# The last addition of the rotary step and the sums of the branch projections on VectorE instead of GpSimd

## The chip, the core and the metric

The kernel runs on one core of a Trainium2 chip. The core has a matrix engine (TensorE, PE in the rows, with its weight loads as PEld), VectorE (DVE), ScalarE (ACT), GpSimd (POOL) and a queue that issues the DMAs (SyncE, SP). Each engine works through its own list of instructions in order, and semaphores make one engine wait for another. The metric is the time of one execution on the device in microseconds (us), as the median of several runs.

## What is computed

Two layers of a transformer trunk over 256 tokens of width 1024, all in float32. A layer has a mixer and a mixture of experts (MoE). Cut to what matters here:

```
h = rms_norm(x) * (1 + scale_m(c)) + shift_m(c)
z = h @ w_in                       # q, k, v of three attention branches, and three gates per channel
q, k = apply_rotary(q), apply_rotary(k)      # branches A and C:  x*cos + rotate_half(x)*sin
o_a, o_n, o_d = diff_attention, neighbourhood_attention, dilated_attention
merged = sum over i of sigmoid(gate_i) * (o_i @ w_proj_i)
x = x + gate_m(c) * (merged @ w_out)
h = rms_norm(x) * (1 + scale_f(c)) + shift_f(c)
x = x + gate_f(c) * hier_moe(h)    # 32 experts in 8 groups of 4
```

The six vectors scale, shift and gate of a layer come from silu(c) @ ada_w, which is another large weight matrix to be read.

## The kernel before

**The work.** `mixer` computes z in 15 chunks of 512 columns (`chunk(n)`). A chunk's weights come in two tiles of 1 MB. They are used as pairs of a rounded part and a remainder: `split` makes the rounded part `whi` with ScalarE (L302) and the remainder `wlo` with VectorE (L303), four times a chunk, and `gemm` adds up three products for each (hi*whi, hi*wlo, lo*whi). So PE can't go on in a quarter of a chunk before VectorE has made its `wlo`. Chunks 0 to 8 hold q, k and v, chunks 9 to 14 the gates. Ten pieces of q and k in each layer need the rotary step, `place`: four shifted copies by ScalarE (L461), two products by VectorE (L462, which reads the matmuls' PSUM bank, and L463), and one addition (L464).

**Around it.** During the chunks the modulation vectors are made too: `ada_part` loads 1 MB of ada_w, and VectorE multiplies and adds it up in two instructions on 128x1024 (L166, each followed by a short one that fetches the sum). The attention of the three branches (`diff_attention`, `na_attention`, `dil_attention`) is written ahead of the gate chunks, and the scheduler lays both into each other on PE. A dilated block consists of scores (matmuls into a `misc` bank), a masked maximum by VectorE (L659), an exponential by ScalarE (L661), a scaling by VectorE (L662, L663), four transposes by PE (L560) with a copy by ScalarE (L562), and the product with v; two heads go through together. Then come the projections of the branches (two halves of 512 columns, three branches each), where VectorE multiplies each with its gate (L493) and adds the branches up (L495; in the first half on GpSimd, in the second on VectorE), and `w_out`.

**The MoE.** For each group of four experts eight tiles of 2 MB (`w13`, L718) and four of 2 MB (`w2g`, L735) are loaded and used once. All weights of the kernel pass through one pool of ten pairs of tiles of 2 MB in all; the DMA queue is in order, and a load starts when its tile has been read by whoever used it before.

**The order.** The program is written as above, but a scheduler orders each engine's instructions before the kernel runs, by a model of the time that each takes. Which instruction stands ahead of which on PE, VectorE and ScalarE is thus decided at build time, with the engine that an addition runs on as an input.

The two statements that the change touches are these (`d` and `sh` are 128x512 in SBUF, `m` and `g` too):

```
nc.vector.tensor_mul(v(d), v(z), cos)             # L462
nc.vector.tensor_mul(v(sh), v(sh), sin)           # L463
nc.gpsimd.tensor_add(d, d, sh)                    # L464
...
nc.vector.scalar_tensor_tensor(g if bi else m, g, 1.0, o[i], op0=OP.add, op1=OP.mult)   # L493
if bi:
    (nc.vector if half else nc.gpsimd).tensor_add(m, m, g)                              # L495
```

Of the kernel before, what the change touches and what calls it, by code (L numbers as in the profile page):

```python
# [53 lines left out]
def bc(ap, at, n):  # L54

    a = [list(e) for e in ap.ap]
    a.insert(at, [0, n])
    return bass.AP(tensor=ap.tensor, offset=ap.offset, ap=a)


class Kernel:
# [288 lines left out]
    def mixer(self, l, fill):  # L350

        nc, tc, io = self.nc, self.tc, self.io
# [37 lines left out]
        def work(name):  # L390
            T, o, n = {"E": (T0, 0, 3), "A": (T1, 0, 2), "PT": (T1, 1024, 2), "PD": (T1, 0, 4)}[name]
            i = turn.get(name, 0)
            turn[name] = (i + 1) % n
            return T[:, o + 512 * i:o + 512 * (i + 1)]
# [22 lines left out]
        def chunk(n):  # L417
# [11 lines left out]
            for kind, c0, wd, dst in SEGS[n]:  # L429
                if wd == 512:  # L430
                    z = [self.acc(), self.acc()]
                    prods += self.wide(z)
                    evac += [lambda t=t, z=z, kind=kind, dst=dst:
                             nc.scalar.copy(vdst[kind][:, t, dst:dst + 512], z[t]) for t in range(2)]
                    continue
                z = self.acc()
                if kind in vdst:
                    prods += [(z[:, t * 256:(t + 1) * 256], False, t, slice(c0, c0 + 256), t == 0) for t in range(2)]
                    evac.append(lambda z=z, kind=kind, dst=dst: nc.scalar.copy(
                        vdst[kind][:, :, dst:dst + 256], z.rearrange("p (t n) -> p t n", t=2)))  # L440
                    continue
                prods += self.flipped(z, c0)
                if kind == "g":
                    evac.append(lambda z=z, dst=dst: nc.scalar.activation(ga[dst // 2], z, AF.Tanh, scale=0.5))
                else:
                    evac.append(lambda z=z, kind=kind, dst=dst: place(z, kind, (qT2 if kind[1] == "q" else kT2)[dst]))
# [6 lines left out]
        def place(z, kind, d):  # L453
            if kind[0] == "n":
                nc.scalar.mul(d, z, 0.125 if kind == "nq" else 1.0)
                return
            cos, sin = (bc(self.rope[:, i, :], 1, 2) for i in range(2))
            v = lambda a: a.rearrange("p (a n) -> p a n", a=2)
            sh = work("PD")
            for q in range(4):  # L460
                nc.scalar.copy(sh[32 * q:32 * q + 32], z[32 * (q ^ 1):32 * (q ^ 1) + 32])  # L461
            nc.vector.tensor_mul(v(d), v(z), cos)  # L462
            nc.vector.tensor_mul(v(sh), v(sh), sin)  # L463
            nc.gpsimd.tensor_add(d, d, sh)  # L464

        for n in range(9):
            chunk(n)
# [15 lines left out]
        for half in range(2):  # L483
            w = [self.slot().rearrange("p (k n) -> p k n", k=4) for _ in range(2)]
            for b in range(2):
                nc.sync.dma_start(w[b], io["w_proj"][l, half, b].rearrange("p (k n) -> p k n", k=4))
            for bi, (k0, nk) in enumerate(srcs):
                o = [self.acc(), self.acc()]
                self.gemm([(k, w[k // 4][:, k % 4:k % 4 + 2]) for k in range(k0, k0 + nk, 2)], hi, lo,
                          self.flipped(o[0], 0) + self.flipped(o[1], 256))  # L490
                for i in range(2):
                    g, m = ga[4 * bi + 2 * half + i], tok[half][:, 512 * i:512 * (i + 1)]
                    nc.vector.scalar_tensor_tensor(g if bi else m, g, 1.0, o[i], op0=OP.add, op1=OP.mult)  # L493
                    if bi:
                        (nc.vector if half else nc.gpsimd).tensor_add(m, m, g)  # L495
        hi, lo = self.to_hilo(None, [tok[i // 2][:, 512 * (i % 2):512 * (i % 2 + 1)].rearrange(
            "p (a n) -> p a n", a=2) for i in range(4)])
        self.gate_row(l, 0)
# [612 lines left out]
```

## Time and profile before

| | |
|---|---|
| median of 3 runs | 1509.85 us (1509.48 to 1510.61) |
| the profiled execution | 1507.89 us |
| its span, first to last instruction | 1506.0 us |
| PE busy | 1198.5 us (80%) |
| VectorE busy | 614.6 us (41%) |
| ScalarE busy | 372.2 us (25%) |
| GpSimd busy | 57.5 us (4%), 67 instructions |
| read from HBM | 542 MB, 361 GB/s over the span |
[...]

The stages follow one another: the first modulation vectors until about 37 us, the mixer of layer 0 until about 332, the MoE of layer 0 until about 774, the mixer of layer 1 until about 1057, the MoE of layer 1 until the end. The share of the span that an engine is busy is a mean over stages of two kinds, so the profile has to be read stage by stage.

### The profile page before, as it was taken

How to read it: one execution, taken by the hardware profiler on the slowest of the kernel's cores; microseconds unless marked ns; L12 is line 12 of the kernel's file. 1: busy time of each engine (PE TensorE's matmuls, PEld its weight loads, DVE VectorE, ACT ScalarE, POOL GpSimd, SP SyncE). 2: the span in 40 equal slices, each digit the busy share in tenths (PEclk: the TensorE clock that was granted, in tenths of full speed). 3: DMA queues.
4: the chain of work that ended last, by engine and by line, in shares of the span. 5: the costliest groups of instructions: out<-in, count | busy, mean ns of one | idle time of the engine just before them, and what ended most of it. 6: DMA issues, size and time to landing. Idle time of an engine off the chain costs nothing. (4 is left out here: it accounts for less than half of the span.)

```text
span 1506.0 us, 19652 instructions
## 1 busy us (share of the span) xinstructions
PE 1198.5 (80%) x8146; PEld 787.0 (52%) x8146; DVE 614.6 (41%) x1246; ACT 372.2 (25%) x664; POOL 57.5 (4%) x67
## 2 busy tenths in 40 slices
PE   2999998989877676676778999999787578577675
PEld 2898987874333132231358989889443133133132
DVE  6889974572121021110149997457322112022012
ACT  2765554350000000000046656544100000000001
POOL 0102000100000000000001110010000000000001
PEclk7999998899988897897999999999998888798898
DMA  9887971769999999999996965276999999999997
GB/s 373 351 348 279 380 293 57 298 254 390 427 428 427 427 427 428 429 427 428 424 416 280 390 276 221 113 284 247 365 426 429 426 430 426 427 429 427 429 428 296
DMA packets 53084, 544.43 MB, mean 362 GB/s; under 512 B 7168, under 2 KB 8192, under 8 KB 12160
## 3 DMA queue, kind: packets, MB, share of 16 engines
q1 hardware_dynamic: 52992, 543.13, 86.9%
q8 instruction: 66, 1.08, 0.3%
q14 instruction: 26, 0.21, 0.0%
HBM read 542.04 MB, written 1.06 MB: 361 GB/s over the span
## 5 line engine op out<-in xcount | busy, mean ns | idle before, releaser
L95 PE MATMUL acc<-rg,xg 128*32 128x512 f32 x2048 | 282.0, 694 | 115.6 <-DMA rg<-w 113.5
L95 PE MATMUL acc<-rg,b 128*32 128x512 f32 (+1 forms) x1152 | 153.0, 662 | 95.9 <-DMA rg<-w2g 69.2
L95 PEld LDWEIGHTS acc<-rg,xg 128*32 128x32 f32 x2048 | 68.6, 119 | 304.3 <-issue 295.1
L95 PE MATMUL acc<-hi,wlo 128*128 128x256 f32 x704 | 200.2, 289 | 7.9 <-DVE wlo L303 7.7
L95 PE MATMUL acc<-lo,whi 128*128 128x256 f32 x704 | 196.1, 284 | 0.0
L95 PE MATMUL acc<-hi,whi 128*128 128x256 f32 x704 | 191.4, 286 | 1.2 <-ACT whi L302 1.1
L303 DVE TENSOR_TENSOR wlo<-rg,whi 128x1024 fp32r<-128x1024 f32 x116 | 145.0, 1250 | 59.1 <-ACT whi L302 58.1
L813 DVE TENSOR_TENSOR b<-b,acc 128x512 f32<-128x512 f32 x16 | 11.0, 688 | 353.1 <-PE acc L95 353.1
L302 ACT CAST whi<-rg 128x1024 fp32r<-128x1024 f32 x116 | 121.5, 1047 | 107.4 <-PE acc L95 99.2
L95 PEld LDWEIGHTS acc<-hi,wlo 128*128 128x128 f32 x704 | 135.1, 192 | 15.3 <-DVE wlo L303 11.6
L95 PEld LDWEIGHTS acc<-rg,b 128*32 128x32 f32 x1152 | 33.9, 120 | 197.1 <-DMA rg<-w2g 105.1
L95 PEld LDWEIGHTS acc<-lo,whi 128*128 128x128 f32 x704 | 134.5, 192 | 1.4 <-issue 1.0
L95 PEld LDWEIGHTS misc<-b,xn 128*128 128x128 f32 x512 | 124.6, 334 | 16.9 <-issue 15.5
L95 PEld LDWEIGHTS acc<-hi,whi 128*128 128x128 f32 x704 | 131.0, 192 | 2.9 <-ACT whi L302 2.1
L95 PE MATMUL misc<-b,xn 128*128 128x128 f32 x512 | 125.6, 404 | 3.9 <-DVEq L918 2.0
L166 DVE CUSTOM_DVE_ANT_0 rg<-rg,grb 128x1024 f32<-128x1024 f32 x96 | 118.6, 1274 | 10.0 <-DMA rg<-ada_w 9.8
L812 ACT ACTIVATE b<-acc 128x512 f32<-128x512 f32 x16 | 9.6, 597 | 440.7 <-PE acc L95 440.7
L826 DVE TENSOR_TENSOR Y<-acc,grb 128x512 f32<-128x512 f32 x28 | 19.4, 692 | 228.2 <-PE acc L95 228.2
L793 DVE TENSOR_SCALAR xg<-misc,mcol 128x128 f32<-128x128 f32 x128 | 44.3, 405 | 106.5 <-PE misc L95 106.5
L806 ACT COPY b<-misc 128x256 f32<-128x256 f32 x16 | 6.0, 373 | 329.2 <-PE misc L805 329.2
L95 PE MATMUL acc<-hi,rg 128*128 128x256 f32 x384 | 74.6, 293 | 13.1 <-ACT hi L265 12.1
L95 PEld LDWEIGHTS acc<-hi,rg 128*128 128x128 f32 x384 | 62.7, 201 | 14.4 <-ACT hi L265 12.6
(168 smaller groups left out, 1437.0 us busy)
## 6 DMA issues: line engine op xcount, KB each, us to landing
rg<-w SPq DMA_DIRECT2D x128, 2048.0 KB, 39.1
rg<-w2g SPq DMA_DIRECT2D x56, 2048.0 KB, 38.9
rg<-w_in SPq DMA_DIRECT2D x56, 1024.0 KB, 9.8
rg<-ada_w SPq DMA_DIRECT2D x48, 1024.0 KB, 8.3
rg<-w2c SPq DMA_DIRECT2D x12, 1024.0 KB, 26.8
rg<-w_proj SPq DMA_DIRECT2D x8, 1024.0 KB, 7.1
rg<-w_out SPq DMA_DIRECT2D x8, 1024.0 KB, 5.8
rg<-w_in SPq DMA_DIRECT2D x8, 512.0 KB, 14.9
```

The lines of the kernel that those rows point to most:

```text
L95: return self.nc.tensor.matmul(out, lhsT, rhs, start=start, stop=stop, **kw)
L166: self.nc.vector.tensor_tensor_reduce(w, w, self.grb, scale=1.0, scalar=0.0, op0=OP.mult, op1=OP.add, accum_out=to)
L302: keep(nc.scalar.copy(whi, w))
L303: keep(nc.vector.tensor_sub(wlo, w, whi.bitcast(F32)))
L793: nc.vector.tensor_scalar(xg[:, k, :], p[:, kk * P:(kk + 1) * P], gf[:, k:k + 1], sf[:, k:k + 1], op0=OP.mult, op1=OP.add)
L806: nc.scalar.copy(ST, p[:, :256])
L812: nc.scalar.activation(a, h1, AF.Silu)
L813: nc.vector.tensor_mul(a, a, h3)
L826: nc.vector.tensor_mul(Y[:, hs], y[half], self.grb[:, hs])
```

## The change

Both additions are made by VectorE, in both layers: 10 rotary additions (L464) and 4 sums (L495) a layer, 28 instructions in all. GpSimd keeps its small fills (L214, L372) and the products of the final normalization (L773).

```
@@ place, in mixer
-            nc.gpsimd.tensor_add(d, d, sh)
+            nc.vector.tensor_add(d, d, sh)
@@ mixer, the projections
-                        (nc.vector if half else nc.gpsimd).tensor_add(m, m, g)
+                        nc.vector.tensor_add(m, m, g)
```

The scheduler puts the instructions of the mixers into another order with it. On VectorE in chunks 5 to 7 of layer 0 (L166 are the ada_w sums, `wlo_1043` and `wlo_1140` are remainders of a quarter of w_in, `rg<-rg 128x1024` those of quarters that have their home elsewhere):

```order
 L462 TENSOR_TENSOR rg<-acc,rg 128x512
 L463 TENSOR_TENSOR rg<-rg 128x512
-L462 TENSOR_TENSOR rg<-acc,rg 128x512
-L463 TENSOR_TENSOR rg<-rg 128x512
-L166 ISA rg,sums<-rg,grb 128x1024
-L166 ISA sums 128x1
-L166 ISA rg,sums<-rg,grb 128x1024
-L166 ISA sums 128x1
+L166 ISA rg,sums<-rg,grb 128x1024
+L166 ISA sums 128x1
+L166 ISA rg,sums<-rg,grb 128x1024
+L166 ISA sums 128x1
+L462 TENSOR_TENSOR rg<-acc,rg 128x512
+L463 TENSOR_TENSOR rg<-rg 128x512
+L464 TENSOR_TENSOR rg<-rg 128x512
 L303 TENSOR_TENSOR wlo_1043<-rg,whi_1042 128x1024
```

One addition stands there ahead of `wlo_1043`, and the second rotary pair has moved behind two sums.

On VectorE in layer 1, from the second rotary product of chunk 1 on, before:

```order
L463 TENSOR_TENSOR rg<-rg 128x512
L166 ISA rg,sums<-rg,grb 128x1024
L166 ISA sums 128x1
L166 ISA rg,sums<-rg,grb 128x1024
L166 ISA sums 128x1
L303 TENSOR_TENSOR wlo_5130<-rg,whi_5129 128x1024
L303 TENSOR_TENSOR rg<-rg 128x1024
L303 TENSOR_TENSOR wlo_5199<-rg,whi_5198 128x1024
```

and with the change:

```order
L463 TENSOR_TENSOR rg<-rg 128x512
L166 ISA rg,sums<-rg,grb 128x1024
L166 ISA sums 128x1
L166 ISA rg,sums<-rg,grb 128x1024
L166 ISA sums 128x1
L303 TENSOR_TENSOR wlo_5130<-rg,whi_5129 128x1024
L464 TENSOR_TENSOR rg<-rg 128x512
L303 TENSOR_TENSOR rg<-rg 128x1024
L464 TENSOR_TENSOR rg<-rg 128x512
L303 TENSOR_TENSOR wlo_5199<-rg,whi_5198 128x1024
```

Both additions of the chunk stand behind the remainder `wlo_5130`.

On PE at the end of the attention of layer 0, where the last quarter of the gates (`whi_2485`) is used up, before (the L560 rows are transposes, the rows from 64x128 on the products with v and the next block's scores):

```order
L95 MATMUL acc<-hi,whi_2485 128x256
L95 MATMUL acc<-hi,wlo_2486 128x256
L95 MATMUL acc<-lo,whi_2485 128x256
L560 MATMUL misc<-k_72,rg 128x128 x8
L95 MATMUL misc<-rg 64x128
L95 MATMUL misc<-rg 128x256
L95 MATMUL misc<-rg 128x128 x2
L95 MATMUL misc<-rg 64x128 x7
```

and with the change:

```order
L560 MATMUL misc<-k_72,rg 128x128 x4
L95 MATMUL acc<-lo,whi_2485 128x256
L95 MATMUL acc<-hi,whi_2485 128x256
L95 MATMUL acc<-hi,wlo_2486 128x256
L560 MATMUL misc<-k_72,rg 128x128 x4
L95 MATMUL acc<-lo,whi_2485 128x256
L95 MATMUL acc<-hi,whi_2485 128x256
L95 MATMUL acc<-hi,wlo_2486 128x256
L95 MATMUL acc<-lo,whi_2485 128x256
L95 MATMUL misc<-rg 64x128
L95 MATMUL misc<-rg 128x256
```

The eight transposes of the second dilated block stood behind the gates' last matmul and now stand among the gates' matmuls. Two more blocks follow in both orders. In layer 1 the end of the attention is in the same order as before.

## Rows read from the trace of the kernel before

**Rows 1.** Busy time of each engine in five stretches, with granted clock and DMA.
```profile
core 0: us, PE busy (x) PEld busy (x) DVE busy (x) ACT busy (x) POOL busy (x), PEclk, DMA share, GB/s
40.00:248.00 208.00, 201.28 (x1504) 187.06 (x1503) 174.48 (x331) 119.36 (x207) 18.12 (x12) 0.99 0.76 304
248.00:278.00 30.00, 23.48 (x110) 17.59 (x110) 9.04 (x23) 11.12 (x25) 0.00 (x0) 0.54 0.24 89
...
345.00:770.00 425.00, 310.45 (x1939) 129.38 (x1930) 64.23 (x141) 16.02 (x37) 0.63 (x9) 0.88 1.01 427
780.00:995.00 215.00, 210.10 (x1593) 195.26 (x1593) 165.33 (x309) 127.52 (x223) 18.16 (x12) 0.99 0.64 254
```

**Rows 2.** The chain that ended last, share of the span by engine.
```profile
DMA 23%; PE 1%; DVE 0%; ACT 0%; issue 0%; SPq 0%; ACTq 0%
```

**Rows 3.** SP's waits from 190 to 350 us: total, times, longest.
```profile
SPq L718 <- DVE wlo L303: 31.1, 3, 11.8
```

**Rows 4.** GpSimd's additions, by line: shortest, median, longest in ns, first and last start.
```profile
L464 POOL TENSOR_TENSOR rg<-rg x20: 1282/2133/2145, 56.1 to 887.0; 128x512 f32<-128x512 f32 x20
...
L495 POOL TENSOR_TENSOR rg<-rg x8: 1286/1784/2301, 286.5 to 1015.3; 128x512 f32<-128x512 f32 x8
```

**Rows 5.** VectorE in order of time from 100 us: start, duration, instruction.
```profile
100.08 0.68 DVE L463 TENSOR_TENSOR rg<-rg 128x512 f32<-128x512 f32 x1
100.68 1.22 DVE L166 CUSTOM_DVE_ANT_0 rg<-rg,grb 128x1024 f32<-128x1024 f32 x1
...
101.83 2.31 DVE L166 CUSTOM_DVE_ANT_0 rg<-rg,grb 128x1024 f32<-128x1024 f32 x1
```

**Rows 6.** VectorE in order of time: first and last stretched instruction, each layer.
```profile
59.34 2.31 DVE L303 TENSOR_TENSOR wlo<-rg,whi 128x1024 fp32r<-128x1024 f32 x1
...
145.75 1.56 DVE L187 TENSOR_TENSOR rwg<-rwg,mcol 128x320 f32<-128x320 f32 x1
...
803.53 2.31 DVE L166 CUSTOM_DVE_ANT_0 rg<-rg,grb 128x1024 f32<-128x1024 f32 x1
...
875.19 2.31 DVE L303 TENSOR_TENSOR rg<-rg 128x1024 fp32r<-128x1024 f32 x1
```

**Rows 7.** PE in order of time, where it waited for VectorE's remainders.
```profile
61.70 0.39 PE L95 MATMUL acc<-hi,wlo 128*128 128x256 f32 x1 [0.44 <-DVE wlo L303]
...
74.53 0.50 PE L95 MATMUL acc<-wlo,hi 128*128 128x512 f32 x1 [0.30 <-DVE wlo L303]
...
133.53 0.39 PE L95 MATMUL acc<-hi,wlo 128*128 128x256 f32 x1 [2.01 <-DVE wlo L303]
...
195.43 0.39 PE L95 MATMUL acc<-hi,wlo 128*128 128x256 f32 x1 [0.93 <-DVE wlo L303]
...
807.04 0.39 PE L95 MATMUL acc<-hi,wlo 128*128 128x256 f32 x1 [2.44 <-DVE wlo L303]
...
820.87 0.50 PE L95 MATMUL acc<-wlo,hi 128*128 128x512 f32 x1 [1.29 <-DVE wlo L303]
```

**Rows 8.** PE in order of time, end of the attention of layer 0.
```profile
248.06 0.60 PE L560 MATMUL misc<-k,rg 128*128 128x128 f32 x4
252.30 1.09 PE L560 MATMUL misc<-k,rg 128*128 128x128 f32 x4 [3.64 <-DVE rg L663]
253.32 6.59 PE L95 MATMUL misc<-rg 128*64 128x128 f32 x28
...
262.36 1.08 PE L560 MATMUL misc<-k,rg 128*128 128x128 f32 x4 [1.41 <-DVE rg L663]
...
277.51 0.36 PE L95 MATMUL acc<-hi,whi 128*128 128x256 f32 x1
```

**Rows 9.** PE in order of time, the same matmuls late in layer 1.
```profile
988.94 1.50 PE L95 MATMUL misc<-rg 128*64 128x128 f32 x8
992.46 2.16 PE L95 MATMUL misc<-rg 128*64 128x128 f32 x20
```

**Rows 10.** VectorE in order of time, one remainder among the projections.
```profile
290.38 2.03 DVE L303 TENSOR_TENSOR wlo<-rg,whi 128x1024 fp32r<-128x1024 f32 x1 [0.28 <-ACT whi L302]
```

## The prediction

> **What bounds the kernel now.** I read the busy time by stage first, because the page's totals mix two kinds of stage. In the MoE of layer 0 the DMA engines are full, at 427 GB/s, while PE is busy 310 of 425 us; in the mixers PE is busy 201 of 208 and 210 of 215 us while DMA has room [rows 1]. The chain that ended last names only DMA, but it covers the last quarter of the span alone [rows 2]; it says what ends the kernel, not what delayed it. The bytes are fixed, so the MoE stages can't be shortened by this change. They can only start earlier. SP's waits say whether they would: the first MoE tiles (L718) wait until the mixer's remainders have been made and its tiles are free [rows 3]. So a microsecond that PE gains in a mixer moves everything behind it, and the question is what holds PE up there.
>
> VectorE holds it up. It is busy 174 of 208 us in mixer 0 [rows 1], and PE's waits in the first chunks end on a remainder `wlo` from VectorE: 0.44, 0.30, 2.01 and 0.93 us in layer 0, 2.44 and 1.29 in layer 1 [rows 7]. [...]
>
> **What an addition costs on either engine.** On GpSimd it takes 1.28 us at its shortest and 2.13 at the median [rows 4]. On VectorE the same shape starts 0.60 us ahead of the next instruction (100.08 to 100.68) and is 0.68 us long with the overlap [rows 5]. So 10 rotary additions are 6.0 us of VectorE's time a layer, and 4 sums are 2.4.
>
> Against that stands what GpSimd takes from VectorE. Wherever a rotary addition runs there, one of VectorE's instructions is stretched: the sum at 101.83 takes 2.31 us, the one right ahead of it 1.22 [rows 5]. There are 8 stretched ones in each layer, from 59.34 to 145.75 and from 803.53 to 875.19 [rows 6]; their excess over the usual length of each adds up to 6.8 us in layer 0 (five of 1.06 to 1.09, then 0.78, 0.54 and 0.07) and 7.3 in layer 1. VectorE's own load thus stays where it is: 6.0 for 6.8, and 6.0 for 7.3.
>
> **Part one, the rotary additions in layer 0.** What changes is which instruction pays. A stretch falls on whatever comes next, often a remainder or a sum right ahead of one; the new additions mostly stand behind the remainders. The remainder that ends the 0.44 us wait is itself stretched (59.34), by 1.09 us: that wait goes. Up to the 0.30 us wait two stretches of 1.09 leave and three additions of 0.60 come, so that goes as well. From 99 us on VectorE has next to no idle time until the 2.01 us wait: stretches of 1.09, 0.07, 1.09 and 0.78 leave, and three additions come, 3.03 - 1.80 = 1.2 us earlier. Sum: 0.44 + 0.30 + 1.2 = 1.9. VectorE sets the pace again at 195.43, and as a whole it has gained only 0.8 us by then, plus what it idles less when PE is ahead. The lower bound is 0.8. The upper one is all three waits, 2.75. I take **1.8**, between them and near the sum, because VectorE has idle time to give up (174 of 208 us busy).
>
> **Part two, the same in layer 1.** The stretched sum at 803.53 stands ahead of `wlo_5130`; both additions stand behind it. The wait of 2.44 loses 1.1. Ahead of the wait of 1.29 a stretch of 0.79 and one of 1.08 leave; PE arrives 1.1 earlier, and the remainder 1.9 earlier, so 0.8 of that wait goes. Together **1.9**; bounds 1.3 (VectorE's net) and 3.7 (both waits).
>
> **Part three, the end of the attention of layer 0.** This is the order's doing and the largest term. Before, PE ran out of gate matmuls at 248.06 and had three sets of transposes ahead of it; the second half of the first set waited 3.64 us for VectorE, and only at 253.32 came the next products [rows 8]. With the change that set stands among the gate matmuls. The stretch from 248.06 to 253.32, 5.26 us, goes, and the eight transposes cost 1.2 us elsewhere (0.60 for four at full clock): 4.1. That is the lower bound if the rest, 253.32 to 277.51, stays as slow. The rest ran at the low clock: 28 matmuls took 6.59 us, and the same 8 and 20 take 1.50 + 2.16 = 3.66 at full clock [rows 8, 9]. The wait of 3.64 stands at the start of the slow stretch. If it was what brought the clock down, the first 28 now find the full clock: 2.9 more, 7.0. If it holds to the end, two blocks take 3.66 + 3.5 each (3.5 is the softmax from 259.9 to 263.4, which the clock doesn't shorten) and the last transposes and products (4.0 is left of the 24.2 after two blocks of 6.59 + 3.5; halved, as an estimate) 2.0: 16.3 in place of 24.2, and the gain is 12.0. A wait of 1.41 us, and one like it in the next block, stand in that stretch [rows 8], so I expect the clock to fall there all the same. I take the middle of 4.1 and 7.0, **5.5**.
>
> **Part four, the sums of the projections.** One remainder there takes 2.03 us in place of 1.22 [rows 10], which GpSimd's addition explains; that goes, and PE was held up a little by it. But two additions, 1.2 us, now stand ahead of another remainder that has little room, and may cost as much. **0**, bounds -0.5 and +0.5 a layer. GpSimd's code setup moves to its first product at the end of the kernel (L773), where it has been idle for long; nothing waits.
>
> **The sum.** 1.8 + 1.9 + 5.5 + 0 = 9.2 us. The profiled execution would go from 1507.89 to 1498.7; it lies 2.0 below the median, so the median goes from 1509.85 to **1500.7**.
>
> **Rivals.**
>
> *VectorE becomes the bound* (the slower side). Where it has no idle time, from 95 to 155 us and from 846 to 888, six additions stand in each layer. If the stretches had another cause than GpSimd's additions, or fell on others instead, VectorE would be 3.6 us later in each, PE would wait for remainders, and the softmaxes of layer 0 would be late too, so that the end of the attention gains nothing: 1509.85 + 7.2 = 1517.0. It decides as soon as an addition costs VectorE more than it gives back, that is if less than 0.60 us of stretch leaves for each. The rows speak against it: the stretches stand only beside GpSimd's additions, and are longer in sum. [...] Chance 0.09.
>
> *The attention gains nothing.* The transposes stand earlier, but PE waits there for a softmax as it did at 252.30, only elsewhere. For it: the chain of a block (maximum, exponential, scaling) is serial and as long as before. Against it: 33 gate matmuls or more stand between a block's scores and its transposes in the new order, some 4.4 us at 201 us for 1504 [rows 1], and the softmax from 259.9 to 263.4 took 3.5 with the second half of the transposes in it [rows 8]. Parts one and two remain: 3.7, 1506.1. Chance 0.16.
>
> *The clock holds.* Parts one and two and 12.0: 15.7, 1494.2. For it: in layer 1 PE passes the same place without falling, with one block of transposes left over there. Against it: two blocks are left here. Chance 0.19.
>
> *The gain doesn't arrive.* DMA takes it back: the chunks draw 304 GB/s in layer 0 [rows 1], with full stretches, and a PE that is ahead would wait for w_in instead of a remainder; or the order that I read isn't the one that counts. 1509.9. Against it: a mean of 0.76 leaves room. Chance 0.12.
>
> **How the numbers follow.** The forecast has 0.44; its own range, from the terms' bounds, is 1495.5 to 1503.7. For 8 in 10 I leave out the slower case (0.09) and the lower half of the case in which the clock holds (0.1): 1494.0 to 1510.5. A measurement of this kernel can tell about 0.2%, or 3 us, from no change, so faster means below 1506.8. Faster: 0.44 + 0.19 + 0.10 of the third case, which lies at the border, 0.73. Same: 0.06 + 0.12 = 0.18. Slower: 0.09.
>
> **What the profile after would show.** Part one and two: no instruction of VectorE above 1.4 us in the mixers, L464 on VectorE at 0.68; the waits at 133.53 and 807.04 halved, those of 0.44 and 0.30 gone. Part three: no wait of 3 us or more ahead of the transposes at the end of the gates of layer 0, and from the last gate matmul to the first projection 20 to 25 us in place of 29.5. Part four: no change from 278 to 330 us but the start. MoE stages as long as before, at 427 GB/s. The forecast is wrong if VectorE's busy time in the mixers grows by more than 2 us a layer, if PE's clock falls in a new place, or if the MoE of layer 0 starts less than 5 us earlier.

## The result, and the profile after

| | before | after |
|---|---|---|
| median | 1509.26 us (1506.92 to 1510.61) | 1492.49 us (1490.26 to 1499.79) |
| ratio, 95% interval | | 0.9896 [0.9876, 0.9916] |
| profiled execution, its span | 1507.89, 1506.0 us | 1490.26, 1488.5 us |
| VectorE busy | 614.6 us | 613.7 us |
| GpSimd busy | 57.5 us | 7.4 us |

By the medians the change makes the kernel faster by 16.8 us. I had said 9.2, and 1492.49 lies 1.5 us below the lower end of my range, 1494.0.

The same views of the changed kernel follow. First busy time by stage (engines, granted clock, DMA), which answers [rows 1]:

```profile
core 0: us, PE busy (x) PEld busy (x) DVE busy (x) ACT busy (x) POOL busy (x), PEclk, DMA share, GB/s
40.00:246.40 206.40, 200.66 (x1518) 186.71 (x1517) 174.32 (x344) 120.49 (x211) 0.13 (x2) 1.00 0.77 307
246.40:262.30 15.90, 12.05 (x98) 9.31 (x98) 7.74 (x19) 9.12 (x21) 0.00 (x0) 1.00 0.30 109
...
332.00:760.00 428.00, 309.56 (x1946) 129.66 (x1945) 66.92 (x155) 19.07 (x44) 0.73 (x10) 0.89 1.01 427
765.00:979.00 214.00, 211.27 (x1604) 196.09 (x1604) 164.00 (x323) 129.61 (x227) 0.13 (x2) 1.00 0.65 257
```

The second row is the news. The end of the attention of layer 0 took 30 us at a granted clock of 0.54 [rows 1]; it now takes 15.9 us at 1.00, the full clock all through. VectorE's load in the chunks is what it was, 174.3 us, and the MoE still runs at 427 GB/s.

PE in order of time, where it waits for remainders in the chunks (in brackets the wait and who ended it), which answers [rows 7]:

```profile
131.09 0.38 PE L95 MATMUL acc<-hi,wlo 128*128 128x256 f32 x1 [0.40 <-DVE wlo L303]
194.40 0.39 PE L95 MATMUL acc<-hi,wlo 128*128 128x256 f32 x1 [2.96 <-DVE wlo L303]
789.60 0.39 PE L95 MATMUL acc<-hi,wlo 128*128 128x256 f32 x1 [1.35 <-DVE wlo L303]
802.33 0.50 PE L95 MATMUL acc<-wlo,hi 128*128 128x512 f32 x1 [0.83 <-DVE wlo L303]
```

The waits of 0.44 and 0.30 are gone, 2.01 is down to 0.40, 2.44 to 1.35 and 1.29 to 0.83. But 0.93 has become 2.96: PE arrives there 3.1 us earlier and finds VectorE only 1.0 earlier (195.43 before, 194.40 now). Behind the wait of 2.01 the clock had fallen for a moment (granted 0.88 from 130 to 135); in this profile of the changed kernel it is 1.00 all through the chunks of layer 0.

VectorE's instructions by line (busy, mean ns), and the rotary additions by themselves (shortest, median, longest in ns):

```profile
L303 DVE TENSOR_TENSOR wlo<-rg,whi 128x1024 fp32r<-128x1024 f32 x116 | 141.9, 1223 | 59.4 <-ACT whi L302 58.3 <-DMA rwg<-rw 0.4 <-DMA rg<-ada_w 0.3
L166 DVE CUSTOM_DVE_ANT_0 rg<-rg,grb 128x1024 f32<-128x1024 f32 x96 | 113.4, 1221 | 7.6 <-DMA rg<-ada_w 7.6
L464 DVE TENSOR_TENSOR rg<-rg x20: 682/686/693, 56.4 to 869.7; 128x512 f32<-128x512 f32 x20
```

No stretched instruction is left: the longest of VectorE in the mixers takes 1.27 us, where [rows 6] had 2.31.

PE in order of time at the end of the attention of layer 0, from the last gate matmul to the first projection, which answers [rows 8]:

```profile
246.17 0.28 PE L95 MATMUL acc<-lo,whi 128*128 128x256 f32 x1
246.38 3.59 PE L95 MATMUL misc<-rg 128*64 128x128 f32 x28
251.45 0.63 PE L560 MATMUL misc<-k,rg 128*128 128x128 f32 x4 [1.48 <-DVE rg L663]
252.42 0.63 PE L560 MATMUL misc<-k,rg 128*128 128x128 f32 x4 [0.34 <-DVE rg L663]
252.98 3.59 PE L95 MATMUL misc<-rg 128*64 128x128 f32 x28
256.99 0.63 PE L560 MATMUL misc<-k,rg 128*128 128x128 f32 x4 [0.42 <-DVE rg L663]
259.22 0.63 PE L560 MATMUL misc<-k,rg 128*128 128x128 f32 x4 [1.60 <-DVE rg L663]
...
262.16 0.36 PE L95 MATMUL acc<-hi,whi 128*128 128x256 f32 x1
```

The 28 matmuls that took 6.59 us [rows 8] take 3.59, both times. The wait of 3.64 is gone, and the first projection stands at 262.16, 15.35 us earlier than before.

SP's waits, finally, show that the MoE still starts when the remainders are done, as in [rows 3] (total, times, longest), so what a mixer gains arrives:

```profile
SPq L718 <- DVE wlo L303: 31.3, 3, 12.1
```

### The profile page after: what moved, and what is told of

It is laid out like the page before. It is cut to its first block, busy times and chain, and to the rows that moved or that the text cites. A ratio compares the mean times of both kernels' runs of the same rounds, so it can differ in the third digit from the quotient of the medians.

```text
span 1488.5 us, 19603 instructions
## 1 busy us (share of the span) xinstructions
PE 1183.2 (79%) x8146; PEld 777.9 (52%) x8146; DVE 613.7 (41%) x1274; ACT 371.8 (25%) x664; POOL 7.4 (1%) x39
## 5 line engine op out<-in xcount | busy, mean ns | idle before, releaser
L95 PE MATMUL acc<-rg,xg 128*32 128x512 f32 x2048 | 276.8, 682 | 118.1 <-DMA rg<-w 116.1
L303 DVE TENSOR_TENSOR wlo<-rg,whi 128x1024 fp32r<-128x1024 f32 x116 | 141.9, 1223 | 59.4 <-ACT whi L302 58.3
L166 DVE CUSTOM_DVE_ANT_0 rg<-rg,grb 128x1024 f32<-128x1024 f32 x96 | 113.4, 1221 | 7.6 <-DMA rg<-ada_w 7.6
```

Source lines behind the costliest of these rows:

```text
L95: return self.nc.tensor.matmul(out, lhsT, rhs, start=start, stop=stop, **kw)
L166: self.nc.vector.tensor_tensor_reduce(w, w, self.grb, scale=1.0, scalar=0.0, op0=OP.mult, op1=OP.add, accum_out=to)
L303: keep(nc.vector.tensor_sub(wlo, w, whi.bitcast(F32)))
```

## The experiments

The times of the stages are what most experiments are read by, so they stand here together, each from PE's rows of one profile. "Chunks" runs from the mixer's first product to the end of its last gate matmul, "bare end" from there to the first projection, "between" from the first projection of layer 0 to the first product of layer 1, "rest" from the last gate matmul of layer 1 to the end. All in us.

| profile | chunks 0 | bare end 0 | between | chunks 1 | rest |
|---|---|---|---|---|---|
| before | 214.18 | 29.28 | 501.39 | 217.71 | 509.4 |
| after | 212.12 | 15.71 | 500.38 | 215.64 | 510.3 |
| rotary additions only | 213.09 | 15.71 | 500.56 | 215.56 | 510.5 |
| sums only | 214.16 | 28.87 | 500.40 | 218.33 | 509.2 |
| layer 0 only | 213.76 | 20.51 | 500.29 | 218.45 | 511.7 |
| layer 1 only | 214.63 | 29.53 | 500.86 | 215.98 | 510.1 |
| after, once more | 214.55 | 20.53 | 501.20 | 215.61 | 510.3 |
| after, scores held | 213.07 | 30.45 | 500.89 | 215.61 | 511.8 |
| after, additions on GpSimd too | 221.32 | 16.80 | 501.67 | 222.12 | 509.6 |
| before, one wait filled | 214.15 | 25.41 | 500.58 | 218.69 | 509.6 |
| before, three waits filled | 214.47 | 20.63 | 501.13 | 218.82 | 509.4 |
| after, two waits filled | 213.60 | 15.71 | 500.48 | 215.68 | 510.0 |
| the same once more | 214.32 | 15.71 | 500.47 | 215.66 | 510.1 |
| the same, sums on GpSimd | 213.90 | 15.71 | 501.26 | 215.70 | 511.1 |

**Each part alone.** By the profiles each of these has, in the mixer of layer 0 up to the projections, the order of the changed kernel where the rotary addition is on VectorE, and otherwise that of the kernel before. So it is in layer 1, but for one: with the rotary additions only, VectorE and PE have an order of their own there, and the chunks still take 215.56 us.

Rotary additions only:

```
-            nc.gpsimd.tensor_add(d, d, sh)
+            nc.vector.tensor_add(d, d, sh)
```

> Only the 20 rotary additions (L464) are made by VectorE; the sums of the projections (L495) stay on GpSimd. In layer 0 every engine's order up to the projections is that of the changed kernel. Theory A (the whole gain is made ahead of the projections, most of it at the end of the attention of layer 0): 1492 to 1495 us, with the first projection of layer 0 at about 262 and no instruction of VectorE above 1.4 us in the chunks, but one stretched remainder left among the projections. Rival B (the sums carry a part that I had put at 0): 1497 us or more.

Measured: 1492.22 us, ratio 0.9903 [0.988, 0.9925]. The rotary additions carry the gain.

Sums of the projections only:

```
-                        (nc.vector if half else nc.gpsimd).tensor_add(m, m, g)
+                        nc.vector.tensor_add(m, m, g)
```

> Only the 8 sums of the first halves of the projections (L495) are made by VectorE; every engine's order stays that of the kernel before. Theory A: within 1.5 us of the kernel before, about 1509; the stretched remainder of 2.03 us is down to 1.22 and the two additions cost about as much. Rival B: the sums are worth 4 us or more, 1505.

Measured: 1509.49 us, 1.0011 [1.0002, 1.0021], a loss of 0.3 to 3.2 us by the interval, although the three stretched remainders that each layer had there (1.41, 2.03 and 1.39 us) are gone. The sums by themselves gain nothing.

Layer 0 only, and layer 1 only:

```
+            (nc.gpsimd if l else nc.vector).tensor_add(d, d, sh)
...
+            (nc.vector if l else nc.gpsimd).tensor_add(d, d, sh)
```

(the sums likewise)

> Both additions are made by VectorE in layer 0 alone; in layer 0 every engine's order is that of the changed kernel, in layer 1 that of the kernel before. Theory A (parts one and three): 16.0 of the 18 us that the profiled executions differ by are there when the MoE of layer 0 starts, so 1493 to 1496 us. Rival B (a gain in layer 0 is waited away by the MoE, and layer 1 carries it): 1503 or more.

> Both additions are made by VectorE in layer 1 alone; in layer 0 every engine's order is that of the kernel before. Theory A (part two alone): 1.0 to 2.5 us less than the kernel before, 1507 to 1508.5, with the wait ahead of the remainder at 807 halved. Rival B (layer 1 carries most): 1500 or less. Rival C (nothing of part two arrives, since the MoE takes it back): 1509.3.

Measured: 1495.62 us, 0.9911 [0.9894, 0.9927], and 1507.22 us, 0.9988 [0.9978, 0.9997]: by the ratios 13.4 and 1.8 us less. Together 15.2, where the rotary additions of both layers gave 14.6 and the whole change 15.7. Within the intervals (1.4 to 3.4 us to either side) the layers add up; that the figures lie closer than that is luck, with four executions in two of the sets. The profile of layer 0 alone brought a surprise: its order is that of the changed kernel, but its bare end took 20.51 us and not 15.71, since the clock had fallen in the middle (granted 0.71 from 246 to 264). That raised the question whether the changed kernel itself can end in both ways.

**The changed kernel once more**, unaltered.

> The changed kernel once more. Theory A (its executions differ by whether the clock holds at the end of the attention of layer 0, a matter of 5 us, and at the start of the MoE stages): most runs at 1490 to 1494, some up to 1500, median 1492 to 1494. Rival B (the first runs were a lucky set): median above 1496.

Measured: 1497.64 us (1490.00 to 1500.94), 0.9917 [0.9897, 0.9937]. That is rival B's median, above 1496: the first set was in part a lucky one, though the fastest execution here is 1490.0 too. PE in order of time in its profile, the same place as above:

```profile
248.57 3.59 PE L95 MATMUL misc<-rg 128*64 128x128 f32 x28
253.64 0.63 PE L560 MATMUL misc<-k,rg 128*128 128x128 f32 x4 [1.48 <-DVE rg L663]
254.61 1.09 PE L560 MATMUL misc<-k,rg 128*128 128x128 f32 x4 [0.34 <-DVE rg L663]
255.62 6.59 PE L95 MATMUL misc<-rg 128*64 128x128 f32 x28
...
269.17 0.36 PE L95 MATMUL acc<-hi,whi 128*128 128x256 f32 x1
```

The first 28 matmuls take 3.59 us as above. Behind the wait of 1.48 the clock falls (granted 0.74 from 246 to 264); the second 28 take 6.59 us, and the first projection comes 4.8 us later behind the last gate matmul. So the same program ends in two ways. Of the twelve executions of the changed kernel in both sets, seven took 1490.0 to 1494.7 us and five 1497.5 to 1500.9; the profiled ones among them, 1490.26 with the clock held and 1498.06 with it fallen, belong to either group; of the other ten only the time is known. The median of all twelve is 1494.2. The two profiles are 7.8 us apart, of which the bare end makes 4.8 and the chunks of layer 0 make 2.4: in this profile the clock fell for a moment behind the wait of 2.96 as well (granted 0.89 from 190 to 205, where the first profile has 1.00).

**Is it the wait that lets the clock fall?** In the kernel before, four products that nobody reads fill the wait of 3.64 us, pinned between the two sets of transposes (this edit and others below are written out more plainly than they stand in the kernels):

```
@@ dil_attention, behind the transposes of the first head
+    for _ in range(4 if len(pts) == 1 and (l, hp, tq) == (0, 0, 1) else 0):
+        self.tc.keep_in_program_order(self.mm(junk, kT[0][:, 0, :P], qT[0], True, True))
@@ pt, first transpose of the second head
+    self.tc.keep_in_program_order(t)
```

> The kernel before, with four more products on TensorE (float32, 128x512, into a PSUM bank that nobody reads) placed between the two sets of transposes of the second dilated block of layer 0, that is into its wait of 3.64 us. Every other instruction of that stretch stays in its order. Theory A (PE standing still for 3.6 us is what lets the clock fall there, and the low clock is worth 9 us): the next 28 matmuls take 3.6 us in place of 6.59, the first projection comes 7 to 10 us earlier, at 268 to 271, and the time is 1499 to 1502 us. Rival B (the clock falls for what runs there, and not for the wait): the 28 matmuls take 6.6 us as before and the time is 1508 to 1510.

Measured: 1504.25 us, 0.9968 [0.9956, 0.9981], between the ranges of the two theories. PE in order of time (each of the four products is two instructions):

```profile
248.38 3.60 PE L95 MATMUL adap<-rg 128*128 128x512 f32 x8
252.19 0.63 PE L560 MATMUL misc<-k,rg 128*128 128x128 f32 x4 [0.21 <-DVE rg L663]
252.75 3.59 PE L95 MATMUL misc<-rg 128*64 128x128 f32 x28
256.70 0.63 PE L560 MATMUL misc<-k,rg 128*128 128x128 f32 x4 [0.36 <-DVE rg L663]
258.88 0.63 PE L560 MATMUL misc<-k,rg 128*128 128x128 f32 x4 [1.55 <-DVE rg L663]
259.44 6.52 PE L95 MATMUL misc<-rg 128*64 128x128 f32 x28
```

With the wait filled the next 28 matmuls take 3.59 us: the wait it was. But behind the next long wait, 1.55, the clock falls all the same, and of the 7 to 10 us at the first projection only 3.9 came (the bare end went from 29.28 to 25.41). So the later waits were filled as well, with one product each:

```
-    for _ in range(4 if len(pts) == 1 and (l, hp, tq) == (0, 0, 1) else 0):
+    for _ in range({(0, 0, 1): 4, (0, 1, 0): 1, (0, 1, 1): 1}.get((l, hp, tq), 0) if len(pts) == 1 else 0):
```

> The kernel before, with four products in the wait of 3.64 us, as in the run before, and one more in each of the two later waits (1.41 and 1.47 us, which grew to 1.55). Additions and order are those of the kernel before. Theory A (those two waits let the clock fall there a little later): the clock holds to the first projection, which comes at 268 to 270, and the time is 1499 to 1501 us; what then remains to the changed kernel with its clock held, 7 to 9 us, is order and additions. Rival B (the clock falls there whatever fills the waits): 1504, as with the first wait filled alone.

Measured: 1500.24 us (1499.80 to 1500.34), 0.9941 [0.9925, 0.9958].

```profile
253.07 3.59 PE L95 MATMUL misc<-rg 128*64 128x128 f32 x28
...
259.20 0.63 PE L560 MATMUL misc<-k,rg 128*128 128x128 f32 x4 [0.69 <-DVE rg L663]
259.76 3.59 PE L95 MATMUL misc<-rg 128*64 128x128 f32 x28
...
269.07 0.36 PE L95 MATMUL acc<-hi,whi 128*128 128x256 f32 x1
```

The clock holds to the first projection (granted 1.00 from 248 to 278), and six products of no use make the kernel before 8.8 us faster. The bare end goes from 29.28 to 20.63: 8.65 us is what the low clock cost there. What the change's order saves beyond that is 20.63 - 15.71 = 4.9, of which 1.2 are transposes that went into the chunks.

**Does the order carry part three, or GpSimd's silence?** The changed kernel, with the scores of the second dilated block held behind the fourth gate matmul from the end, about where they were before; the products ahead of them go along (`gates` are the gate chunks' matmuls, `held` the six scores and the six products ahead of them):

```
+        if (l, n) == (0, 14):
+            for i in held:
+                tc.add_manual_dep(i.ins, gates[-4].ins.name, no_sync, reason="held")
```

> The changed kernel, with the scores of the second dilated block of layer 0 held back until four matmuls ahead of the end of the gates, where the kernel before had most of them; its transposes then stand behind the gates again. All additions are on VectorE. Theory A (the order at the end of the attention carries part three): PE waits 3 us or more ahead of the second set of transposes, the 28 matmuls behind it take 6.6 us, the first projection is at 272 to 277 and the time 1503 to 1508 us. Rival B (VectorE without GpSimd's additions beside it carries it, and the order does not): no such wait, the 28 matmuls take 3.6 us and the time is 1493 to 1496.

Measured: 1504.96 us, 0.9976 [0.9967, 0.9986].

```profile
251.44 1.94 PE L560 MATMUL misc<-k,rg 128*128 128x128 f32 x8 [4.13 <-DVE rg L663]
...
253.31 6.59 PE L95 MATMUL misc<-rg 128*64 128x128 f32 x28
```

With all additions on VectorE, a wait of 4.13 us is back, the clock falls (granted 0.54 from 248 to 278), and the bare end takes 30.45 us. The order carries all of part three. 3.8 us remain, from the chunks.

And the other way round, the changed kernel with GpSimd's additions beside VectorE's:

```
-            nc.vector.tensor_add(d, d, sh)
+            nc.vector.tensor_add(d, d, sh); nc.gpsimd.tensor_add(sh, d, sh)
```

> The changed kernel, with one addition of 128x512 on GpSimd behind each of the 20 rotary additions, whose result nobody uses (into the shifted copy, which is dead by then). The order on PE, VectorE and ScalarE is that of the changed kernel but for two places of a few instructions, so VectorE has its own additions and GpSimd's beside it. Theory A (the order carries part three; the stretches beside GpSimd's additions carry parts one and two): stretched instructions of VectorE are back, 6 to 7 us a layer in sum, the mixers' chunks are 2 to 4 us longer each, and from the last gate matmul to the first projection it is 16 or 20.6 us as in the two profiles of the changed order; 1498 to 1503 us. Rival B (the stretches carried part three as well): 25 us or more there and 1506 to 1512. Rival C (the stretches cost nothing): 1491 to 1497.

Measured: 1506.24 us, 0.998 [0.9962, 0.9998]. The time missed theory A's 1498 to 1503 and lies in rival B's range, but not for rival B's reason. The bare end is 16.80 us, where rival B has 25 or more, so part three is there nearly in full (the 1.1 us above 15.71 came with a clock that fell late, granted 0.51 from 270 to 273). But against the mean of the changed order's other profiles (213.6 and 215.7) the chunks are longer by 7.7 us in layer 0 and by 6.4 in layer 1, where I had expected 2 to 4. The stretches are back: eight of VectorE's instructions in layer 0 and ten in layer 1 are 1.1 us longer than their kind, 8.7 and 10.9 us in all (two more in layer 0 add 0.9). By line, and the additions themselves:

```profile
L166 DVE CUSTOM_DVE_ANT_0 rg<-rg,grb 128x1024 f32<-128x1024 f32 x96 | 123.1, 1318 | 9.0 <-DMA rg<-ada_w 8.9
L464 DVE TENSOR_TENSOR rg<-rg x20: 674/678/1783, 56.5 to 888.6; 128x512 f32<-128x512 f32 x20
L464 POOL TENSOR_TENSOR rg<-rg x20: 1301/2130/3248, 57.3 to 889.4; 128x512 f32<-128x512 f32 x20
```

VectorE's sums of ada_w have a mean of 1318 ns in place of 1221, and its own additions reach 1783. PE pays a large part of what GpSimd's additions take from VectorE: its waits for VectorE in the chunks add up to 10.5 us in layer 0 and 7.0 in layer 1, against 5.6 and 2.2 in the profile after. In layer 0 the clock fell behind two of them besides (2.79 and 2.95 us; granted 0.89 from 145 to 160 and 0.87 from 197 to 210). No engine waits for GpSimd's additions themselves by more than 0.2 us. The two rotary products of the kernel before differ beside GpSimd's additions:

```profile
L462 DVE TENSOR_TENSOR rg<-acc,rg x20: 676/685/692, 54.6 to 885.5; 128x512 f32<-128x512 f32 x20
L463 DVE TENSOR_TENSOR rg<-rg x20: 674/681/1473, 55.2 to 886.2; 128x512 f32<-128x512 f32 x20
```

L463, with both inputs in SBUF, reaches 1473 ns, and L462, which reads one from PSUM, never more than 692, although eight of its twenty ran beside an addition on GpSimd. No run changed where an input lies.

**The changed kernel with its longest waits filled**, with one product that nobody reads in each of its two longest waits (1.48 and 1.60 us):

```
+    at = (l, hp, tq, len(pts)) in ((0, 1, 0, 0), (0, 1, 1, 1))
+    if at:
+        self.tc.keep_in_program_order(self.mm(junk, kT[0][:, 0, :P], qT[0], True, True))
```

> The changed kernel, with one more product on TensorE (float32, 128x512, into a PSUM bank that nobody reads) in each of the two longest waits of PE at the end of the attention of layer 0 (1.48 and 1.60 us); no other instruction moves there. Theory A (in the slower executions of the changed kernel, as in the profile of the run with layer 0 alone, the clock falls in that stretch, and it starts from those waits): all runs within 3 us of each other, the median 1 to 2 us below the changed kernel's, 1490 to 1492. Rival B (the runs differ for another reason): the same scatter of 1490 to 1500 and the same median of 1492.5.

> The changed kernel with the two products in TensorE's waits once more, for more executions. Theory A (the waits of 1.48 and 1.60 us decide whether the clock falls): all runs at 1490 to 1494.5. Rival B (four fast ones by chance, where about half of the changed kernel's are): some at 1497 to 1501.

Measured: 1491.78 us (1491.31 to 1494.11), 0.9894 [0.988, 0.9908], and 1491.48 us (1489.40 to 1492.17), 0.988 [0.9863, 0.9896]. Beside the first of the two ran the changed kernel itself, at 1497.64; the intervals of the two ratios overlap. PE in order of time in the second profile:

```profile
253.29 0.63 PE L560 MATMUL misc<-k,rg 128*128 128x128 f32 x4 [0.43 <-DVE rg L663]
...
254.82 3.59 PE L95 MATMUL misc<-rg 128*64 128x128 f32 x28
...
261.07 0.63 PE L560 MATMUL misc<-k,rg 128*128 128x128 f32 x4 [0.75 <-DVE rg L663]
```

The waits are down to 0.43 and 0.75, the bare end is 15.71 us, and of eight executions none is above 1494.11, where five of the changed kernel's twelve are at 1497.5 or more. In both profiles the clock still falls for a moment behind the wait of 2.97 in the chunks, which nothing fills (granted 0.96 from 160 to 200 in the second); their chunks take 213.60 and 214.32 us. That the two products make the end even is borne out by this; how much they gain in the median is not settled, since only four executions ran beside six of the changed kernel.

The same with the sums left on GpSimd:

```
-                        nc.vector.tensor_add(m, m, g)
+                        (nc.vector if half else nc.gpsimd).tensor_add(m, m, g)
```

> The rotary additions on VectorE, the sums of the projections on GpSimd, and the two products in TensorE's waits at the end of the attention of layer 0: what the runs so far point to as best. Theory A: the sums cost VectorE 1 to 1.6 us in both layers together, so 1489.5 to 1491.5, with no run above 1494.5. Rival B (the sums make no difference here): the same median as the changed kernel with the two products, 1491.8.

Measured: 1493.27 us (1491.37 to 1494.41), 0.9894 [0.9877, 0.991]; 1.8 us more than with the sums on VectorE beside it, where I had expected less. The two intervals overlap, so whether the sums on VectorE gain anything in this order stays open. With this the waits were filled in twelve executions, and in the profiles of all three runs the clock held at the end of the attention (granted 1.00 from 246 to 264).

## Why the prediction was wrong, point by point

**Part three is the step that failed**: "so I expect the clock to fall there all the same. I take the middle of 4.1 and 7.0". I had worked out three values, by where the clock falls. The lowest, 4.1, has not been seen once: in all seven profiles of the changed order the first 28 matmuls run at full clock (3.59 us in six, and granted 1.00 from 246 to 264 in the seventh). In two it falls behind them; the bare end is then 8.8 us shorter than before, and less the 1.2 for the transposes that went into the chunks that is 7.6, where I had 7.0 for that case. In five it holds to the end (three of these with waits partly filled): 13.6 - 1.2 = 12.4, where I had 12.0. So the terms were right within 0.6 us and the choice among them was not. I took a point between two cases, which is no case at all, and gave a chance of 0.19 to the one that, by their times, 7 of 12 executions belong to. Its own forecast, 1494.2, was 1.7 us off. The range went wrong with it, since its lower end leaves out half of that case on purpose. How far off it looks is in part luck: the six executions of the result have more of the short ends than the six that came later, and the median of all twelve, 1494.2, would stand just inside the range, with the step as wrong as before. The rows that I had didn't decide it: a wait of 1.41 us stood in a stretch where the clock was low already [rows 8], and can't show whether such a wait lowers a clock that is high.

**Part one**: 1.8 was taken. The mean of the chunks of layer 0 is 214.3 us over the five profiles of the old order and 213.6 over the seven of the new one without extra additions or held scores, and the latter hold 1.2 us of transposes more: 0.7 + 1.2 = 1.9. The waits of 0.44 and 0.30 went, and 1.6 of the 2.01 where I had worked out 1.2; but a new one of 2.96 came at 194.40, since VectorE sets the pace there; up to it the gain is 1.0 (1.3 from the mixer's first product on), close to the lower bound, which was VectorE's net. The new order's profiles differ by 2.4 us among themselves, and the clock goes with it: in the two in which it stays up behind this wait the chunks take 212.6 us on the mean, in the five in which it falls there 214.0. The gain is thus 2.9 or 1.5. A clock that falls in a new place was one of my own signs that the forecast is wrong, and with the profile of the held scores it came in six of eight. The stretches are beside eight of the ten additions in each layer and not, as I wrote, wherever one runs.

**Part two**: 1.9 was taken, 2.7 measured: 218.4 us for the chunks of layer 1 over the five profiles with the old order there (217.7 to 218.8), 215.7 over eight with the new (215.6 to 216.0). The wait of 2.44 lost 1.09 (1.1 was said), the one of 1.29 lost 0.46 (0.8 was said); the remainder was gained elsewhere in the chunks, where I didn't trace it.

**Part four**: 0 is not refuted, but the bounds, 1 us for both layers, were tight: +1.7 us in the old order by the ratio (0.3 to 3.2), and -1.8 in the new by two medians whose intervals overlap. The recorded range of 1495.5 to 1503.7 counts these bounds at its lower end and leaves them out at its upper, which would be 1504.7. GpSimd's setup (MODIFY_POOL_CONFIG, two instructions of 11 ns) went from L464 at 1.1 us to L773 at 1065.1, and no engine waits for it.

**What I had left out**: with the rotary additions of layer 1 on VectorE the stretch from its last gate matmul to the end takes 510.0 to 511.8 us in eight profiles, against 509.2 to 509.6 in four of five with them on GpSimd alone (511.7 in the fifth, that of layer 0 alone). So about half a microsecond or more of part two is given back. It goes with the clock at the start of the MoE of layer 1: from 30 to 90 us behind the last gate matmul the granted clock is 0.91 to 0.92 in all nine profiles with 510.0 us or more, and 0.94 in the other five, among them the one with additions on both engines (509.6). That one causes the other wasn't tried. The two largest, 511.7 and 511.8, have 1.0 and 1.1 us of it ahead of the projections, where the clock fell in these two profiles alone (granted 0.97 from 985 to 1050 in both).

**The rivals.** "The clock holds" is what the first profile shows, and by the times most executions of the first set. "VectorE becomes the bound" had the mechanism right and the sign of the balance wrong: with both GpSimd's and VectorE's additions the chunks grow, by 7.7 and 6.4 us; with VectorE's alone they don't, because the stretches that leave, 6.8 and 7.3 us, outweigh the 6.0 that come. "The attention gains nothing" is the run with the scores held: 3.8 us remained, and 3.7 had been worked out for it. "The gain doesn't arrive" fell: the stretch between the layers' mixers takes 500.3 to 501.7 us in all profiles.

## What to carry to other kernels

Where a wait of TensorE lies in a stretch at low clock, or ahead of one, work out the stretch at both levels (here 3.59 and 6.59 us for the same 28 matmuls) as separate cases, and give each its chance; here bare ends of 15.7 and 20.5 us came, and a forecast in the middle of two cases is that of neither. Look for long waits in stretches where TensorE has nothing else queued: filling those of 1.4 to 3.6 us with products of no use was worth 8.8 us in the kernel before, and the twelve executions of the changed kernels with two such products stay within 5.1 us of each other (1489.40 to 1494.41), where twelve without are 10.9 apart. And before work is handed to GpSimd, look for VectorE's instructions that are longer beside it than elsewhere; here each addition handed over cost VectorE about as much time as making it (6.8 and 7.3 us of stretches for ten additions, against 6.0).

## What the runs showed of the hardware

One program, in one order, ends with the clock held or fallen behind the same waits of 1.48 and 0.34 us (bare ends of 15.71 and 20.53 us). No run here shows what decides between the two.

The length of one wait alone doesn't say what will happen. A wait of 3.64 or 4.13 us at that place had a low clock behind it in each of four profiles (granted 0.54 to 0.60 from 248 to 278 us). Behind the wait of 2.96 us (2.95 to 2.98) in the chunks of the changed order the granted clock stayed at 1.00 in two profiles and fell in six, as these rows of the profile after and of the second one with two waits filled show (160 to 200 us; the clock is the third number from the end):

```profile
160.00:200.00 40.00, 36.16 (x280) 33.59 (x280) 38.09 (x90) 19.96 (x42) 0.00 (x0) 1.00 0.91 367
...
160.00:200.00 40.00, 36.16 (x267) 33.48 (x266) 37.24 (x90) 19.42 (x42) 0.00 (x0) 0.96 0.91 367
```

Behind the wait of 2.01 us in the chunks of the old order it fell in three profiles of five (granted 0.89 from 130 to 145 us, and 1.00 in the other two).
